# A four-layer float32 decoder trunk on one core: a third deferred column block, another opening order, the last conv chunk without copies, and equal offsets for high and low rows

## The chip, the cores and the metric

The kernel runs on one core of a Trainium2 chip. The metric is the time of one execution on the device in microseconds (us); less is better.

## What is computed

A trunk of four layers over one sequence of 256 rows of 1024 features, float32 throughout. Layer i's mixer is attention (0 and 3), a convolution module (1) or RWKV-7 (2); each is followed by a gated FFN of 2816 hidden units. Each sub-layer is normalised and modulated by six vectors from the conditioning vector c:

```python
for i in range(DEPTH):
    mod = (silu(c) @ ada_w[i] + ada_b[i]).reshape(B, 6, D)
    h = rms_norm(x, norm_mix_g[i]) * (1 + scale_m) + shift_m
    x = x + gate_m * mixer[i % 3](h)
    h = rms_norm(x, norm_ffn_g[i]) * (1 + scale_f) + shift_f
    x = x + gate_f * ((silu(h @ ffn_w_gate[i]) * (h @ ffn_w_up[i])) @ ffn_w_down[i])

def conformer_conv_mixer(h, ...):
    u = glu(h @ w_pw1 + b_pw1)
    u = causal_depthwise_conv(u, w_dw) + b_dw        # 31 taps per channel
    u = layer_norm(u, ln_g, ln_b)
    return silu(u) @ w_pw2 + b_pw2
```

## The kernel before

x lies in SBUF as 8 chunks of 128 features by 256 rows and stays there. Weights come once from HBM, 1 MB at a time, by DMAs issued on SP; each half (128x1024) is split into a high part `wh` (cast to fp32r on ScalarE, ACT, L272) and a low part `wl` = raw - wh (on VectorE, DVE, L273). Activation rows are split in the same way into a high and a low set (`xh`, `xl`; in the FFN's second half `hh`, `hl`). Each exact product is three fp32r passes into one PSUM tile, `wh.xh`, `wh.xl`, `wl.xh` (`mm3`, L289 to L291, with the rows moving and the weights stationary; `mm3t`, L300 to L302, in attention, with the weights moving). Some small products stay float32 in one matmul, which the trace shows as two records.

*Order.* The tile framework's scheduler orders instructions on each engine by the order of the code and by priorities; `issue_after(ins)` keeps an instruction behind another one. `pace` and `pump` spread the steps of c @ ada_w (128x1024 each, L228 on DVE) between the weight blocks.

*Rows and sets.* `new_set` makes a high and a low tile (2048 floats + 48); there are set 0 and set 1. `self.shift` = 16 * i, set by layer i's FFN, moves the place of the rows within them (`chunks`), and the same 16 * i is used in `hh` and `hl`. By this layout the high and the low rows lie 192 bytes apart modulo 1024 in set 1 and in `hh`/`hl`.

*FFN* (`ffn`, L1226). 22 column blocks f, each with a gate half and an up half (24 matmuls each), then 8 output chunks (`w_down`). The first `DEFERRED` = 2 blocks behind a mixer run on rows that aren't yet normalised (set 0; 256 columns and 2 that carry the shift); their results are multiplied by the norm's factor r (L1249, L1252). Meanwhile the normalised rows are built on DVE and ACT into set 1 (L1263 to L1265), which the other blocks use.

*Opening* (`__init__`, `opening`). The first modulation vectors are needed before the first matmul: 512 KB halves of ada_w come in pairs, then x, then more. DVE multiplies each by silu(c). Half the chunks (0 to 3) are scaled, shifted and used in float32 matmuls (L409), while DVE computes the other half of the scale; then chunks 4 to 7 follow as inputs (L388 on ACT) and are split for the first fp32r matmuls (L300).

*Conv* (`conv`, L1062). Eight column blocks d of the first projection give chunks `us[d]`. Depthwise taps run two blocks later (`depthwise`, e = d - 2): 24 taps on TensorE (PE) as matmuls with 32-wide diagonals `dg` over four shifted copies `u4`, which go through DRAM (`shifts`, on GpSimd, POOL); one tap with the bias on ACT; 6 on DVE (L1188). `lead` takes chunk 0's y0 off the others; `tally` (L1096) sums y and its squares for the layer norm, a chain of single DVE and ACT instructions at the end.

## Time and profile before

| | |
|---|---|
| three runs | 1824.60, 1827.16, 1830.43 us (median 1827.16) |
| the profiled execution | 1824.64 us, of it span 1822.8 us |
| mean granted TensorE clock | 0.98 |
| busy | PE 95%, DVE 78%, ACT 54%, POOL 18% |
| DMA | 368 MB, mean 202 GB/s |

The profile is of one execution. A page gives busy time by engine, the span in 40 slices and the costliest groups of instructions. Timelines list instructions with start, duration, line, and in brackets how long the engine had idled before and what released it. A record of a matmul lasts longer than the step from one to the next, since matmuls overlap.

### The profile page before, as it was taken

How to read it: one execution, taken by the hardware profiler on the slowest of the kernel's cores; microseconds unless marked ns; L12 is line 12 of the kernel's file. 1: busy time of each engine (PE TensorE's matmuls, PEld its weight loads, DVE VectorE, ACT ScalarE, POOL GpSimd, SP SyncE). 2: the span in 40 equal slices, each digit the busy share in tenths (PEclk: the TensorE clock that was granted, in tenths of full speed). 3: DMA queues.
4: the chain of work that ended last, by engine and by line, in shares of the span. 5: the costliest groups of instructions: out<-in, count | busy, mean ns of one | idle time of the engine just before them, and what ended most of it. 6: DMA issues, size and time to landing. Idle time of an engine off the chain costs nothing.

```text
span 1822.8 us, 36724 instructions
## 1 busy us (share of the span) xinstructions
PE 1739.8 (95%) x14228; PEld 1645.1 (90%) x14228; DVE 1417.8 (78%) x2826; ACT 977.4 (54%) x2334; POOL 328.3 (18%) x483
## 2 busy tenths in 40 slices
PE   4999999999999899999998999999989999999999
PEld 3999899899997699998887888999989999989999
DVE  6899998977888798777868568877788797786554
ACT  4666565754453464446551346544476676675443
POOL 4645534000004400000000000000054442300000
PEclk8999999999999999999998999999999999999999
DMA  8577666576896448776333104777856554534543
GB/s 340 219 243 267 230 234 229 175 254 237 267 332 197 118 176 311 259 261 233 116 120 106 59 1 144 263 256 239 312 180 216 176 183 158 212 128 165 184 163 114
DMA packets 72686, 368.27 MB, mean 202 GB/s; under 512 B 9392, under 2 KB 11568, under 8 KB 47808
## 3 DMA queue, kind: packets, MB, share of 16 engines
q1 hardware_dynamic: 70592, 360.23, 56.7%
q0 software_dynamic: 1920, 5.70, 1.3%
q8 instruction: 112, 1.84, 0.4%
q14 instruction: 62, 0.51, 0.1%
...
## 4 chain that ended last, share of the span: by engine, by line
PE 55%; DVE 6%; ACT 2%; issue 1%; DMA 0%; POOL 0%; DVEq 0%; ACTq 0%; POOLq 0%
PE pmm L290 12%; PE pmm L289 12%; PE pmm L291 12%; PE pmm L300 3%; PE pmm L301 3%; PE pmm L302 3%; PE pmm L823 1%; PE pmm L923 1%; DVE wl L273 1%; PE aux L595 1%; PE aux L945 1%; PE aux L618 1%; PE aux L937 1%; ACT wh L272 1%; DVE dg L867 1%
## 5 line engine op out<-in xcount | busy, mean ns | idle before, releaser
L272 ACT CAST wh<-raw 128x1024 fp32r<-128x1024 f32 (+2 forms) x501 | 490.2, 982 | 510.7 <-PE pmm L290 273.5
L273 DVE TENSOR_TENSOR wl<-raw,wh 128x1024 fp32r<-128x1024 f32 (+2 forms) x501 | 580.6, 1161 | 184.9 <-ACT wh L272 180.0
L289 PE MATMUL pmm<-xh,wh 128*128 128x256 f32 (+1 forms) x1856 | 522.1, 285 | 15.0 <-ACT xh L1264 6.6
L290 PE MATMUL pmm<-xl,wh 128*128 128x256 f32 (+1 forms) x1856 | 525.5, 285 | 0.1
L291 PE MATMUL pmm<-xh,wl 128*128 128x256 f32 (+1 forms) x1856 | 519.6, 282 | 0.4 <-DVE wl L273 0.4
L289 PEld LDWEIGHTS pmm<-xh,wh 128*128 128x128 f32 x1856 | 350.1, 190 | 21.0 <-ACT xh L306 7.7
L290 PEld LDWEIGHTS pmm<-xl,wh 128*128 128x128 f32 x1856 | 351.5, 190 | 2.2 <-issue 0.8
L291 PEld LDWEIGHTS pmm<-xh,wl 128*128 128x128 f32 x1856 | 351.5, 190 | 1.3 <-DVE wl L273 0.8
L300 PE MATMUL pmm<-wh,xh 128*128 128x256 f32 x1104 | 321.1, 291 | 17.7 <-DVE rope L546 6.8
L302 PE MATMUL pmm<-wl,xh 128*128 128x256 f32 x1104 | 312.2, 284 | 0.8 <-DVE wl L273 0.8
L301 PE MATMUL pmm<-wh,xl 128*128 128x256 f32 x1104 | 312.5, 283 | 0.0
L300 PEld LDWEIGHTS pmm<-wh,xh 128*128 128x128 f32 x1104 | 210.6, 191 | 24.5 <-ACT xh L306 5.9
L228 DVE SCALAR_TENSOR_TENSOR adaw<-adaw,csil 128x1024 f32<-128x1024 f32 x178 | 222.0, 1248 | 4.9 <-DMA adaw<-in_ada_w 4.9
L548 POOL TENSOR_TENSOR rope<-rope,rope 128x128 f32<-128x128 f32 x192 | 147.2, 790 | 427.5 <-ACT wh L272 217.7
L301 PEld LDWEIGHTS pmm<-wh,xl 128*128 128x128 f32 x1104 | 211.5, 192 | 0.1
L302 PEld LDWEIGHTS pmm<-wl,xh 128*128 128x128 f32 x1104 | 210.1, 191 | 1.0 <-DVE wl L273 1.0
L290 PE MATMUL pmm<-hl,wh 128*128 128x256 f32 x704 | 199.1, 283 | 0.0
L291 PE MATMUL pmm<-hh,wl 128*128 128x256 f32 x704 | 197.4, 280 | 0.0
L289 PE MATMUL pmm<-hh,wh 128*128 128x256 f32 x704 | 197.3, 280 | 0.0
L291 PEld LDWEIGHTS pmm<-hh,wl 128*128 128x128 f32 x704 | 132.7, 189 | 0.0
L289 PEld LDWEIGHTS pmm<-hh,wh 128*128 128x128 f32 x704 | 132.6, 188 | 0.0
L290 PEld LDWEIGHTS pmm<-hl,wh 128*128 128x128 f32 x704 | 132.3, 188 | 0.0
...
## 6 DMA issues: line engine op xcount, KB each, us to landing
...
```

Source lines behind the costliest of these rows:

```text
L228: nc.vector.scalar_tensor_tensor(w, w, 1.0, self.csil, ALU.mult, ALU.mult, accum_out=t[:, col:col + 1])
L272: nc.scalar.copy(wh[:, :w], raw)
L273: self.anchor = nc.vector.tensor_sub(wl[:, :w], raw, wh[:, :w].bitcast(F32)).ins
L289: nc.tensor.matmul(out, wh[:, a], xh[:, k, :c], start=first and j == 0, stop=False)
L290: nc.tensor.matmul(out, wh[:, a], xl[:, k, :c], start=False, stop=False)
L291: nc.tensor.matmul(out, wl[:, a], xh[:, k, :c], start=False, stop=last and j == n - 1)
L300: nc.tensor.matmul(out, xh[:, k, tok], wh[:, a], start=first and j == 0, stop=False)
L301: nc.tensor.matmul(out, xl[:, k, tok], wh[:, a], start=False, stop=False)
L302: nc.tensor.matmul(out, xh[:, k, tok], wl[:, a], start=False, stop=last and j == n - 1)
L548: nc.gpsimd.tensor_add(o[:, :, a], o[:, :, a], o2[:, :, c])
L595: nc.tensor.matmul(scs[hh][:, c], T[g][0][rows, hp, tok], T[g][1][rows, hp, kt], start=True, stop=True)
L618: nc.tensor.transpose(pt[:, c * P:(c + 1) * P], pr[:, c * P:(c + 1) * P], self.ident)
```

## The change

1. `DEFERRED` is 3: block f=2 also runs on the deferred rows. The normalised set is still built behind f=0.
2. x is loaded before the first ada_w pair. The low halves of chunks 0 to 3 come behind the last ada step of the opening; the first weight half of the rest is cast before chunks 6 and 7 are made.
3. The conv's last chunk (7) has no shifted copies: 18 taps are float32 matmuls with full 128x128 diagonals `dgs`, built by 18 ACT instructions at d == 2; one tap and the bias stay on ACT, 12 are on DVE. Its taps run at e == 6, before chunk 6's. In the layer norm the mean's square is taken on ACT from PSUM, and the reciprocal root reads the variance directly, with eps as its bias.
4. `self.shift` is gone; tiles of set 0 have 24 floats of pad, those of set 1 none; `hh` and `hl` have 256 floats of pad and the offset 80, 32, 48, 80 by layer. By this layout `xh` and `xl` of set 1, and `hh` and `hl`, lie at equal places modulo 1024 bytes.

```diff
-DEFERRED = 2
+ALONE = 18
+DEFERRED = 3
...
+        nc.sync.dma_start(x, A["x"])
         steps = pair(0)
-        nc.sync.dma_start(x, A["x"])
...
     def chunks(self, t, cols=S):
-        o = self.shift if cols == S else 0
-        return t[:, o:o + KC * cols].rearrange("p (k s) -> p k s", k=KC)
+        return t[:, :KC * cols].rearrange("p (k s) -> p k s", k=KC)
...
-        return self.xp.tile([P, KC * S + 48], dtype, name=f"x{n}{q}")
+        return self.xp.tile([P, KC * S + (0 if q else 24)], dtype, name=f"x{n}{q}")
...
+        if bias is not None:
+            nc.scalar.activation(r, ps, AF.Abs_reciprocal_sqrt, bias=bias)
+            nc.vector.tensor_scalar_add(v, ps, eps)
...
-        split(range(4))
+        with self.tc.issue_after(self.stepped):
+            split(range(4))
...
-            inputs([k])
+            with self.tc.issue_after(self.cast) if k > 5 else nullcontext():
+                inputs([k])
...
+                if d == 2:
+                    for k in range(ALONE):
+                        nc.scalar.mul(dgs[:, k, :], self.ident, wd[:, KC - 1, k:k + 1])
...
-                    shifted[d] = self.shifts(us[d % 4], eye, w4[:, d], tp, dp, shifted.get(d - 1))
+                    if d < KC - 1:
+                        shifted[d] = self.shifts(us[d % 4], eye, w4[:, d], tp, dp, shifted.get(d - 1))
...
+                    if e == KC - 2:
+                        self.depthwise(us[(KC - 1) % 4], None, wd[:, KC - 1], cv[:, 2, KC - 1:], y[:, KC - 1, :],
+                                       tp, (lead, y0), dgs)
...
+            m2 = tp.tile([P, S], F32, name="val")
+            nc.scalar.activation(m2, sums[0], AF.Square, scale=1.0 / D)
             nc.vector.tensor_scalar_mul(mean, sums[0], 1.0 / D)
-            m2 = tp.tile([P, S], F32, name="val")
-            nc.vector.tensor_mul(m2, mean, mean)
...
-        n_pe = 4 * QUADS
+        n_pe = ALONE if dgs is not None else 4 * QUADS
...
+        if dgs is not None:
+            for k in range(n_pe):
+                nc.tensor.matmul(py, dgs[:, k, :], u[:, k:k + S], start=False, stop=k == n_pe - 1,
+                                 skip_group_check=True)
...
-            self.shift = 16 * i
-            hh, hl = (hp.tile([P, FC * S + 48], F32R, name=n)[:, 16 * i:16 * i + FC * S].rearrange(
+            o = (80, 32, 48, 80)[i]
+            hh, hl = (hp.tile([P, FC * S + 256], F32R, name=n)[:, o:o + FC * S].rearrange(
...
-                if f == DEFERRED - 2:
+                if f == 0:
                     dh, dl = self.new_set(1)
```

How the order of instructions moves, at three places. First DVE in the opening, before (`adaw`, `raw` and `wh` hold halves of ada_w; L228 is a step, L307 a low half, L237 the scale):

```order
L307 TENSOR_TENSOR xl0_95<-xh1_228,xh0_94 128x256
L228 SCALAR_TENSOR_TENSOR adaw_171,mod0_0_152<-adaw_171,csil_82 128x1024
L307 TENSOR_TENSOR xl0_95<-xh1_228,xh0_94 128x256
L228 SCALAR_TENSOR_TENSOR raw_173,mod0_0_152<-raw_173,csil_82 128x1024
L307 TENSOR_TENSOR xl0_95<-xh1_228,xh0_94 128x256 x2
L228 SCALAR_TENSOR_TENSOR raw_173,mod0_0_152<-raw_173,csil_82 128x1024
L235 TENSOR_TENSOR mod0_0_152<-mod0_0_152,adab_92 128x4
L228 SCALAR_TENSOR_TENSOR raw_176,mod0_1_155<-raw_176,csil_82 128x1024 x2
L228 SCALAR_TENSOR_TENSOR wh_179,mod0_1_155<-wh_179,csil_82 128x1024
L228 SCALAR_TENSOR_TENSOR wh_181,mod0_1_155<-wh_181,csil_82 128x1024
L235 TENSOR_TENSOR mod0_1_155<-mod0_1_155,adab_92 128x4
L237 SCALAR_TENSOR_TENSOR gs0_1_157<-mod0_1_155,ng_93 128x4
```

and after:

```order
L227 SCALAR_TENSOR_TENSOR adaw_169,mod0_0_152<-adaw_169,csil_82 128x1024
L227 SCALAR_TENSOR_TENSOR adaw_171,mod0_0_152<-adaw_171,csil_82 128x1024
L227 SCALAR_TENSOR_TENSOR raw_173,mod0_0_152<-raw_173,csil_82 128x1024 x2
L234 TENSOR_TENSOR mod0_0_152<-mod0_0_152,adab_92 128x4
L227 SCALAR_TENSOR_TENSOR raw_176,mod0_1_155<-raw_176,csil_82 128x1024 x2
L227 SCALAR_TENSOR_TENSOR wh_179,mod0_1_155<-wh_179,csil_82 128x1024
L227 SCALAR_TENSOR_TENSOR wh_181,mod0_1_155<-wh_181,csil_82 128x1024
L306 TENSOR_TENSOR xl0_95<-xh1_228,xh0_94 128x256
L234 TENSOR_TENSOR mod0_1_155<-mod0_1_155,adab_92 128x4
L306 TENSOR_TENSOR xl0_95<-xh1_228,xh0_94 128x256
L236 SCALAR_TENSOR_TENSOR gs0_1_157<-mod0_1_155,ng_93 128x4
L306 TENSOR_TENSOR xl0_95<-xh1_228,xh0_94 128x256 x4
```

The four low halves that stood between the steps stand behind the last step, and the scale is made between them.

Second DVE in the first FFN, from the last but two pairs of normalised rows on, before (`h0` and `xl1` are the normalised rows, `wl` low halves of weights, `hl` the low half of a block's result):

```order
L307 TENSOR_TENSOR hl_4570<-h_4749,hh_4569 128x256
L1265 SCALAR_TENSOR_TENSOR xl1_4652<-h0_4669,mod0_3_1590,xh1_4651 128x256
L1265 SCALAR_TENSOR_TENSOR xl1_4652<-h0_4673,mod0_3_1590,xh1_4651 128x256
L1263 SCALAR_TENSOR_TENSOR h0_4677<-x_98,gs0_4_2124,rstd2_4613 128x256
L1263 SCALAR_TENSOR_TENSOR h0_4681<-x_98,gs0_4_2124,rstd2_4613 128x256
L273 TENSOR_TENSOR wl_4835<-raw_4828,wh_4834 128x1024
L1265 SCALAR_TENSOR_TENSOR xl1_4652<-h0_4677,mod0_3_1590,xh1_4651 128x256
L1265 SCALAR_TENSOR_TENSOR xl1_4652<-h0_4681,mod0_3_1590,xh1_4651 128x256
L74 TENSOR_TENSOR xl0_95<-shift2_6129,xh0_94 128x8x2
L672 TENSOR_SCALAR omu_10731<-mu_10729 128x48
L273 TENSOR_TENSOR wl_4897<-raw_4894,wh_4896 128x1024
```

and after (`g` and `u` are block f=2's products with r):

```order
L1270 TENSOR_TENSOR g_4822<-pmm_4772,rstd2_4613 128x256
L1286 SCALAR_TENSOR_TENSOR xl1_4652<-h0_4669,mod0_3_1590,xh1_4651 128x256
L1286 SCALAR_TENSOR_TENSOR xl1_4652<-h0_4673,mod0_3_1590,xh1_4651 128x256
L1284 SCALAR_TENSOR_TENSOR h0_4677<-x_98,gs0_4_2124,rstd2_4613 128x256
L1284 SCALAR_TENSOR_TENSOR h0_4681<-x_98,gs0_4_2124,rstd2_4613 128x256
L306 TENSOR_TENSOR hl_4570<-h_4749,hh_4569 128x256
L1286 SCALAR_TENSOR_TENSOR xl1_4652<-h0_4677,mod0_3_1590,xh1_4651 128x256
L1286 SCALAR_TENSOR_TENSOR xl1_4652<-h0_4681,mod0_3_1590,xh1_4651 128x256
L1273 TENSOR_TENSOR u_4828<-pmm_4797,rstd2_4613 128x256
L272 TENSOR_TENSOR wl_4840<-raw_4833,wh_4839 128x1024
L1274 SCALAR_TENSOR_TENSOR h_4823<-u_4828,pmm_4797,g_4822 128x256
L272 TENSOR_TENSOR wl_4902<-raw_4899,wh_4901 128x1024
```

The low half `wl_4835`, which stood before the last pair of normalised rows, has its counterpart `wl_4840` behind them and behind block f=2's `g` and `u`.

Third ACT at the start of the conv, before (`wh` are the casts of the weight halves of blocks d, `sg` a sigmoid, `part` the tap and bias on ACT):

```order
L272 CAST wh_7140<-raw_7138 128x1024
L1112 ACT_TABLE_LOAD
L1112 ACTIVATE sg_7042<-sg_7042,bg_7040 128x256
L272 CAST wh_7144<-raw_7138 128x1024
L1186 ACTIVATE part_7242<-u0_6959,cv_6949,wd_6951 128x256
L272 CAST wh_7255<-raw_7253 128x1024
L1112 ACTIVATE sg_7121<-sg_7121,bg_7119 128x256
L272 CAST wh_7259<-raw_7253 128x1024
L1186 ACTIVATE part_7358<-u1_6960,cv_6949,wd_6951 128x256
L272 CAST wh_7374<-raw_7372 128x1024
L1112 ACTIVATE sg_7200<-sg_7200,bg_7198 128x256
L272 CAST wh_7378<-raw_7372 128x1024
```

and after (L1110 builds the diagonals):

```order
L271 CAST wh_7166<-raw_7164 128x1024
L1110 ACTIVATE dgs_6978<-ident_87,wd_6956 128x128
L1123 ACT_TABLE_LOAD
L1123 ACTIVATE sg_7050<-sg_7050,bg_7048 128x256
L1110 ACTIVATE dgs_6978<-ident_87,wd_6956 128x128 x11
L1123 ACTIVATE sg_7129<-sg_7129,bg_7127 128x256
L1110 ACTIVATE dgs_6978<-ident_87,wd_6956 128x128 x6
L271 CAST wh_7170<-raw_7164 128x1024
L1207 ACTIVATE part_7268<-u0_6966,cv_6954,wd_6956 128x256
L271 CAST wh_7281<-raw_7279 128x1024
L271 CAST wh_7285<-raw_7279 128x1024
```

Eighteen builds stand between the casts `wh_7166` and `wh_7170` of one column block, where one table load and one sigmoid stood between `wh_7140` and `wh_7144`.

## Rows read from the trace of the kernel before

**Rows 1.** The page: busy time by engine, GB/s by slice, the costliest group of matmuls.

```profile
PE 1739.8 (95%) x14228; PEld 1645.1 (90%) x14228; DVE 1417.8 (78%) x2826; ACT 977.4 (54%) x2334; POOL 328.3 (18%) x483
...
GB/s 340 219 243 267 230 234 229 175 254 237 267 332 197 118 176 311 259 261 233 116 120 106 59 1 144 263 256 239 312 180 216 176 183 158 212 128 165 184 163 114
...
L289 PE MATMUL pmm<-xh,wh 128*128 128x256 f32 (+1 forms) x1856 | 522.1, 285 | 15.0 <-ACT xh L1264 6.6
```

**Rows 2.** Windows in the FFN sections: stretch, busy time and records of each engine, granted clock.

```profile
400.00:460.00 60.00, 60.00 (x515) 60.00 (x514) 42.78 (x60) 28.72 (x44) 0.00 (x0) 1.00 0.72 251
480.00:535.00 55.00, 55.00 (x465) 55.00 (x464) 48.81 (x80) 27.63 (x42) 0.00 (x0) 1.00 0.92 323
700.00:780.00 80.00, 80.00 (x675) 80.00 (x674) 61.14 (x89) 37.49 (x57) 0.00 (x0) 1.00 0.79 272
790.00:845.00 55.00, 55.00 (x470) 55.00 (x469) 42.82 (x65) 27.02 (x49) 0.19 (x1) 1.00 0.84 281
1160.00:1240.00 80.00, 80.00 (x681) 80.00 (x680) 59.54 (x83) 38.09 (x58) 0.00 (x0) 1.00 0.77 268
1260.00:1315.00 55.00, 55.00 (x465) 55.00 (x464) 43.16 (x65) 24.59 (x35) 0.00 (x0) 1.00 0.87 298
1660.00:1740.00 80.00, 80.00 (x676) 80.00 (x675) 46.11 (x58) 37.72 (x57) 0.00 (x0) 1.00 0.51 177
```

**Rows 3.** Timeline of PE, attention of layer 0: start, duration, line; first and last of 95.

```profile
101.50 0.28 PE L301 MATMUL pmm<-wh,xl 128*128 128x256 f32 x1
...
112.57 0.28 PE L302 MATMUL pmm<-wl,xh 128*128 128x256 f32 x1
```

**Rows 4.** Timeline of PE, deferred block of the second FFN: first and last of 82.

```profile
659.55 0.47 PE L289 MATMUL pmm<-xh,wh 128*128 128x258 f32 x1
...
669.30 0.28 PE L291 MATMUL pmm<-xh,wl 128*128 128x258 f32 x1
```

**Rows 5.** Waits of PE over the span: total, times, longest.

```profile
PE pmm L289 <- ACT xh L1264: 6.6, 2, 3.3
```

**Rows 6.** Windows behind a wait of PE, opening and first FFN: columns as in rows 2.

```profile
45.00:50.00 5.00, 3.47 (x16) 3.27 (x17) 4.57 (x9) 4.00 (x9) 5.00 (x9) 0.66 0.50 174
361.00:365.00 4.00, 4.00 (x22) 3.91 (x23) 3.97 (x11) 2.33 (x8) 0.00 (x0) 0.62 0.38 154
```

**Rows 7.** Timeline of DVE, opening and first FFN.

```profile
30.54 0.42 DVE L307 TENSOR_TENSOR xl<-xh,xh 128x256 fp32r<-128x256 f32 x1 [2.03 <-ACT xh L306]
...
367.04 1.21 DVE L273 TENSOR_TENSOR wl<-raw,wh 128x1024 fp32r<-128x1024 f32 x1
368.17 0.87 DVE L1265 SCALAR_TENSOR_TENSOR xl<-h,mod,xh 128x256 fp32r<-128x256 f32 x2
```

**Rows 8.** Timeline of PE, first normalised block of the first FFN.

```profile
360.82 1.01 PE L289 MATMUL pmm<-xh,wh 128*128 128x256 f32 x3 [3.29 <-ACT xh L1264]
```

**Rows 9.** Timeline of PE, opening.

```profile
26.39 8.72 PE L409 MATMUL pmm<-raw,xh 128*128 128x256 f32 x32 [9.07 <-ACT xh L388]
34.95 7.07 PE L409 MATMUL aux<-raw,xh 128*128 128x256 f32 x32
45.77 0.39 PE L300 MATMUL pmm<-wh,xh 128*128 128x256 f32 x1 [3.75 <-ACT wh L272]
```

**Rows 10.** Timeline of ACT, opening and start of the conv layer.

```profile
40.61 1.52 ACT L388 ACTIVATE xh<-xl,mod,gs 128x256 f32<-128x256 f32 x2 [8.88 <-DVE gs L237]
...
545.10 1.04 ACT L272 CAST wh<-raw 128x1024 fp32r<-128x1024 f32 x1
```

**Rows 11.** Groups of ACT instructions by line and shape: busy, mean ns, idle before.

```profile
L711 ACT ACTIVATE xl<-raw,mixgs 128x128 f32<-128x128 f32 x16 | 5.1, 391 | 2.0 <-DMA raw<-in_rwkv_aA 2.0
```

**Rows 12.** Timeline of PE, start and end of the conv layer.

```profile
555.91 0.28 PE L291 MATMUL pmm<-xh,wl 128*128 128x258 f32 x1
...
562.25 1.22 PE L1125 MATMUL pmm<-y,lead 128*128 128x256 f32 x2 [2.25 <-DVE y L1189]
...
621.56 2.80 PE L1183 MATMUL pmm<-u,dg 128*32 128x256 f32 x48 [1.23 <-DMA u<-there]
```

More of the change, by code (lines that the diff above doesn't have):

```diff
@@ L148, in __init__ @@
         self.sets = [None, None]
-        self.shift = 0
         for q in range(2):
@@ L227, in ada_step @@
         with self.tc.issue_after(self.anchor) if self.anchor else nullcontext():
-            nc.vector.scalar_tensor_tensor(
-                w, w, 1.0, self.csil, ALU.mult, ALU.mult, accum_out=t[:, col:col + 1])
+            self.stepped = nc.vector.scalar_tensor_tensor(
+                w, w, 1.0, self.csil, ALU.mult, ALU.mult, accum_out=t[:, col:col + 1]).ins
         if col == 0 and m in (1, 4):
@@ L271, in parts @@
         with self.tc.issue_after(self.hold) if self.hold else nullcontext():
-            nc.scalar.copy(wh[:, :w], raw)
+            self.cast = nc.scalar.copy(wh[:, :w], raw).ins
             self.anchor = nc.vector.tensor_sub(wl[:, :w], raw, wh[:, :w].bitcast(F32)).ins
@@ L311, in rsqrt_table, with rsqrt_mean @@
             self.nc.scalar.preload_act_table_set("abs_reciprocal_sqrt_and_small")
-    def rsqrt_mean(self, ps, n, eps, op=ALU.add, rows=P):
+    def rsqrt_mean(self, ps, n, eps, op=ALU.add, rows=P, bias=None):
         nc = self.nc
         v, r, t = (self.sm.tile([P, S], F32, name=m, bufs=1)[:rows] for m in ("var", "rstd", "nrt"))
-        nc.vector.tensor_scalar(v, ps, 1.0 / n, eps, ALU.mult, op)
-        nc.scalar.activation(r, v, AF.Abs_reciprocal_sqrt)
+        if bias is not None:
+            nc.scalar.activation(r, ps, AF.Abs_reciprocal_sqrt, bias=bias)
+            nc.vector.tensor_scalar_add(v, ps, eps)
+        else:
+            nc.vector.tensor_scalar(v, ps, 1.0 / n, eps, ALU.mult, op)
+            nc.scalar.activation(r, v, AF.Abs_reciprocal_sqrt)
         nc.vector.tensor_mul(t, r, r)
@@ L1071, in conv @@
             nc.sync.dma_start(wd, A["w_dw"])
+            eps = hp.tile([P, 1], F32, name="eps")
+            nc.vector.memset(eps, EPS)
             lead = hp.tile([P, P], F32, name="lead")
@@ L1098, in conv @@
             shifted = {}
+            dgs = hp.tile([P, ALONE, P], F32, name="dgs")
             for d in range(KC + 3):
+                if d == 2:
+                    for k in range(ALONE):
+                        nc.scalar.mul(dgs[:, k, :], self.ident, wd[:, KC - 1, k:k + 1])
                 if d < KC:
@@ L1117, in conv @@
                     nc.vector.scalar_tensor_tensor(us[d % 4][:, W - 1:], val, bv, sg, ALU.add, ALU.mult)
[L1118 removed]
+                    if d < KC - 1:
+                        shifted[d] = self.shifts(us[d % 4], eye, w4[:, d], tp, dp, shifted.get(d - 1))
                 if 1 < d <= KC + 1:
                     e = d - 2
[L1121 to L1122 removed]
+                    if e == KC - 2:
+                        self.depthwise(us[(KC - 1) % 4], None, wd[:, KC - 1], cv[:, 2, KC - 1:], y[:, KC - 1, :],
+                                       tp, (lead, y0), dgs)
+                    if e < KC - 1:
+                        self.depthwise(us[e % 4], shifted.pop(e), wd[:, e], cv[:, 2, e:e + 1],
+                                       y[:, e, :] if e else y0, tp, (lead, y0) if e else None)
                     if e == 0:
@@ L1170, in shifts, with depthwise @@
         return u4, dg, last.ins
-    def depthwise(self, u, shifted, w, bias, y, tp, less):
+    def depthwise(self, u, shifted, w, bias, y, tp, less, dgs=None):
         nc = self.nc
         W = w.shape[-1]
-        n_pe = 4 * QUADS
-        u4, dg, self.copied = shifted
+        n_pe = ALONE if dgs is not None else 4 * QUADS
         py = self.ps.tile([P, 512], F32, name="pmm")[:, :S]
@@ L1180, in depthwise @@
             nc.tensor.matmul(py, *less, start=True, stop=False, skip_group_check=True)
-        for q in range(QUADS):
-            for g in range(4):
-                nc.tensor.matmul(py[32 * g:32 * g + 32, :], dg[:, 4 * q + g, :], u4[:, g, 4 * q:4 * q + S],
-                                 start=q == 0 and not less, stop=q == QUADS - 1, skip_group_check=True)
+        if dgs is not None:
+            for k in range(n_pe):
+                nc.tensor.matmul(py, dgs[:, k, :], u[:, k:k + S], start=False, stop=k == n_pe - 1,
+                                 skip_group_check=True)
+        else:
+            u4, dg, self.copied = shifted
+            for q in range(QUADS):
+                for g in range(4):
+                    nc.tensor.matmul(py[32 * g:32 * g + 32, :], dg[:, 4 * q + g, :], u4[:, g, 4 * q:4 * q + S],
+                                     start=q == 0 and not less, stop=q == QUADS - 1, skip_group_check=True)
         part = tp.tile([P, S], F32, name="part")
```

4 lines of the change are left out of this document (1 added, 3 removed).

## The prediction

> **What bounds the kernel now.** I read the page's busy table first: the reader is to see TensorE (PE) busy for 1739.8 us, 95% of the span [rows 1]. Only two things can therefore shorten the run: the places where PE stands or runs at half clock, and the time of one matmul. For the second I read seven stretches of the feed-forward (FFN) sections, gate/up of all four and down of three, each with PE 100% busy at a granted clock of 1.00 [rows 2]. Counts there include the two or three matmuls that reach over an edge (each record lasts 0.28 us and they start 0.12 us apart), so I take off 2.4. One 128x256 fp32r matmul then takes 117.1 ns in gate/up of the first section (60 / 512.6), 118.9, 117.9 and 118.8 in the next three; in down it takes 118.9, 117.6 and 118.9. The code is the same in the four; what differs is the offset, 16 floats more from section to section, at which the moving rows lie. Offset thus decides up to 1.5% of a matmul's time, and there are 3 x 1856 matmuls with moving x rows [rows 1] and, by the loops of down, 3 x 22 x 8 x 4 = 2112 with moving h rows: 7680. Third, the waits: two of 3.3 us each where an FFN section changes from the deferred rows to the normalised ones, in the sections behind the two attentions [rows 5, 8]; one of 3.75 us in the opening [rows 9]; one of 2.25 us at the conv's start and one of 1.23 at its end [rows 12]. After the first two kinds PE runs for 3 to 4 us at half clock: 1.2 instead of 2.4 GHz, seen as a mean of 0.66 over 45 to 50 us and of 0.62 over 361 to 365 us [rows 6].
>
> **Third deferred block.** DVE is what PE waits for at 360.82: DVE works without a gap and finishes the last pair of normalised low rows at 368.17 + 0.87 = 369.04, while PE runs over them [rows 7]. Before, block f=2 needs those rows; it starts at 360.82 [rows 8], loses 4 x 0.38 = 1.5 us to the clock [rows 6], and with 48 matmuls at 0.118 (5.66 us) blocks f=2 to f=5 end at 368.0, 373.7, 379.3 and 385.0. After, f=2 runs on the deferred rows straight behind f=1 (357.4 to 363.1), so gap and half clock go: 3.3 + 1.5 = 4.8 at most. But PE now comes to the normalised rows while DVE is still at them, and the two extra multiplies by the norm's factor (g and u, 0.43 each as the pair of row operations at 368.17) stand ahead of the low half of f=3's second weight, wl_4840. The last low rows come at 369.04 - 1.2 (the wl that stood ahead of them, at 367.04 [rows 7], now comes behind) + 0.43 = 368.3, the u multiply at 368.7, wl_4840 at 369.9; its 24 matmuls end at 372.7, f=4 at 378.4, f=5 at 384.0. That is 1.0 less; since the matmuls ahead of wl_4840 have then run with PE and its clock up, and the g multiply falls into DVE's earlier pauses at best, I take **1.5 in each of two sections, -3.0**. The two sections behind conv and rwkv don't stand among these waits and are costed at nothing: DVE's work there hides behind PE's. Bounds: -9.6 (both stalls whole) and +1.7 (nothing gained, and 2 x 0.86 us of multiplies on the path).
>
> **Opening.** x (1 MB) is moved ahead of the first two halves of ada_w (1 MB). At the 340 GB/s of the span's first slice [rows 1] these come up to 3.1 us later, x as much earlier. The scale behind them releases PE's first 64 records (32 matmuls), at 26.39 [rows 9]. DVE idles between its first steps, so I take less than half, 1.3 later: 27.7. These matmuls take until 34.95 + 7.07 = 42.02, 15.6 us in all, so they end at 43.3. DVE's second list of ada steps loses four low-half subtractions (0.4 each) and the 2.03 us wait for ACT at 30.54 [rows 7]: 3.7 less, 1.3 more, so the scale that frees ACT at 40.61 [rows 10] comes 2.4 earlier, at 38.2. From there to the first fp32r matmul it was 5.2 us, of which the inputs of chunks 6 and 7 (about 2.1 with their casts) now stand behind the weight's cast: ready at 41.3. PE is then the later one and goes on at 43.3 without standing: 45.77 - 43.3 = 2.5, and the half clock goes with the wait, 5 x 0.34 = 1.7. I take **-4.0**; bounds -5.5 (x's move costs nothing) and +1 (3.1 late, and the wait stays).
>
> **Conv, start.** Eighteen 128x128 diagonals are built on ACT; the nearest row is a 128x128 scaling, 391 ns [rows 11], 7.0 us in all. They stand on ACT between the two weight casts of column block d=2, of which the second, at 545.10, had come with 5 us to spare [rows 10]. After, about 7.6 us stand before it (the builds and two sigmoids): cast near 552.9, its low half near 555.2 on DVE, where PE wanted it at about 553 (the block's last matmul starts at 555.91 [rows 12], its second half is 24 of 0.12). So PE stands 2.1 and then loses some 1.5 to the half clock that follows such a stand [rows 6], 3.6 together; but the 2.25 us that PE waits for DVE's y right behind [rows 12] is then mostly covered. Net **+1.8**; bounds 0 and 7.0.
>
> **Conv, end.** Chunk 7's copies through DRAM go, and with them PE's wait of 1.23 us and 24 small matmuls, 2.80 [rows 12]. Eighteen fp32 matmuls of 128x128 by 256 come; from the opening's rows one takes 7.07 / 16 = 0.44 [rows 9], 7.9 in all, but they need only u, and run ahead of chunk 6's, in the place of waits. Twelve taps on DVE (six before) lie beside them. By my count the last y comes 1.1 later, and the reciprocal root straight from the variance gives 0.25 back: **+0.85**; bounds -1 and +4.2 (7.9 - 2.8 - 1.2, and 0.3 more of waits). POOL's memsets, five DMAs less, and mu's load one section later are covered by POOL's idle 82% of the span [rows 1] and cost nothing; without that cover the third layer's first mixes, which need mu, would start later.
>
> **Addresses.** The high and low rows now lie at equal offsets, where they were 192 bytes apart. No row shows that for moving rows of x or h. In attention the moving operands are the weight's high and low half, which lie at equal offsets: 95 matmuls from 101.50 to 112.57, 117.8 ns each [rows 3]. I take 117.8, as the nearest case, for gate/up from f=3 (19 x 48 x 4 = 3648, mean now 118.2) and for down (2112, mean 118.5): -1.5 and -1.5, **-3.0**. Bounds: at 117.1 -7.0, at 118.9 +3.4.
>
> A rule that speaks against this term: the Trainium skill, "TensorE: Matmul & The Clock Gate", Part 2 (step 1), gives TensorE two independent read ports and says that loading the next tile's weights takes no read bandwidth from the running matmul; no address would matter, the term would be 0 and the sum 3.0 higher. The spread of 117.1 to 118.9 among equal code in [rows 2] speaks against it.
>
> **Sum.** -3.0 - 4.0 + 1.8 + 0.85 - 3.0 = -7.4. The profiled execution took 1824.64 us, so 1817.3 by its own clock; it stands 2.5 below the median of the runs, 1827.16. Against that median the time is 1819.8; I say 1820.
>
> **Rivals.**
> *All matmuls with moving x or h run at 117.1.* Speaks for it: the first section shows that such a place exists. gate/up and down gain 7.0, the other 5568 - 3648 = 1920 (conv, rwkv, deferred blocks) up to 1.5 ns, 2.9: -9.9 for -3.0, so 1813.
> *Addresses do nothing* (equal offsets only shift who is slow): 1823.
> *DVE becomes the bound at the FFN starts.* It is without a gap there [rows 7]; if wl comes later by what f=2 gave, the term is +1.7 for -3.0: 1824.5.
> *Equal offsets are the bad case.* If high and low rows at one offset hinder each other, all 7680 matmuls with moving x or h pay. The slowest long stretch of such matmuls is the deferred block, 81 steps from 659.55 to 669.30, 120.4 ns [rows 4]; against a mean of 118.2 that is +16.9 for -3.0: 1839.7, slower than before. It decides from 118.8 ns on (118.2 + 4.4 us, the gain of all other terms, over 7680); attention's equal weights at 117.8 speak against it.
> *The conv's builds and matmuls stay on the path:* 7.0 + 4.2 for 2.65: 1828.3. That is also where the change fails to do what it says, the copies' wait exchanged for as long a row of matmuls.
>
> **How the numbers follow.** About 0.3%, 5.5 us, is what a measurement of this kernel tells from no change; faster means under 1821.7, slower over 1832.7. Forecast 0.54, own range 1814 to 1825, a good two thirds of it faster (0.39, same 0.15); all at 117.1 0.13, faster; addresses nothing 0.06, same; DVE bound 0.14 (0.12 same, 0.02 slower with a second mishap); bad offsets 0.08, slower; conv on the path 0.05 (0.03, 0.02). Faster 0.52, same 0.36, slower 0.12. The range: from 1806 (the first rival with the opening's best) to 1829 (the conv rival); left out are the bad offsets and tails, 0.15.
>
> **What would show it.** Opening: the first fp32r matmul near 43.3 without an idle bracket, clock 1.00 over 43 to 48. FFN of the first and last layer: 144 matmuls in a row, then short waits for xl and wl, no 0.62. Conv: a wait for ACT's wh or DVE's wl in block d=2; no wait for u from DRAM; 18 matmuls in about 8 us near 614. Addresses: the seven stretches of [rows 2] near 117.8, alike in all layers. I'm wrong if the gap at f=2 reappears whole at f=3, if PE still waits at the first fp32r matmul of the opening, or if the seven stretches move by more than 1 ns on the mean.

## Result and profile after

The changed kernel takes 1801.81 us (median of 4 runs, 1798.57 to 1806.48) against 1827.71 before (4 runs): ratio 0.9861, 95% interval 0.9833 to 0.9889. It was forecast at 1820, with a range from 1806 to 1829: the sign was right, the gain is 26 us instead of 8.

The profiled execution took 1798.57 us. The page's busy line, against [rows 1]: PE is busy for 22.4 us less with nearly the same work.

```profile
PE 1717.4 (96%) x14216; PEld 1623.9 (90%) x14216; DVE 1420.0 (79%) x2840; ACT 984.0 (55%) x2357; POOL 331.7 (18%) x477
```

The windows in the four FFN sections, gate/up, then down, of each. Columns are as in [rows 2]: the stretch, its length, busy time and records of PE, of its weight loads, of DVE, ACT and POOL, then the granted clock, the DMA share and GB/s.

```profile
400.00:455.00 55.00, 55.00 (x488) 55.00 (x487) 40.83 (x56) 27.03 (x41) 1.08 (x1) 1.00 0.70 247
490.00:520.00 30.00, 30.00 (x267) 30.00 (x266) 27.24 (x44) 15.89 (x24) 0.00 (x0) 1.00 0.93 353
700.00:765.00 65.00, 65.00 (x576) 65.00 (x575) 52.40 (x77) 31.97 (x49) 0.00 (x0) 1.00 0.81 281
785.00:825.00 40.00, 40.00 (x335) 40.00 (x335) 30.21 (x46) 17.11 (x28) 0.19 (x1) 1.00 0.85 284
1160.00:1235.00 75.00, 75.00 (x665) 75.00 (x664) 58.05 (x82) 37.43 (x56) 0.00 (x0) 1.00 0.76 263
1255.00:1300.00 45.00, 45.00 (x385) 45.00 (x384) 35.15 (x55) 20.23 (x30) 0.00 (x0) 1.00 0.89 303
1660.00:1725.00 65.00, 65.00 (x576) 65.00 (x575) 39.66 (x51) 32.05 (x48) 0.00 (x0) 1.00 0.52 180
1740.00:1790.00 50.00, 50.00 (x443) 50.00 (x443) 26.35 (x33) 19.54 (x25) 0.00 (x0) 1.00 0.48 162
```

With 2.5 taken off each count (0.28 us over steps of 0.113), a matmul takes 113.3 ns in gate/up of all four sections (55 / 485.5), where it took 117.1 to 118.9, and 113.4 and 113.5 in down of the first and last. In down of the second and third it takes 120.3 and 117.6. None of the rows of before showed a step below 117.

Where the 26 us lie, from starts in the two timelines (x's last update closes a mixer or an FFN; f=5 is taken by its silu on ACT, y0 by its first matmul in PE):

| stage | before | after | difference |
|---|---|---|---|
| to the first fp32r matmul | 45.77 | 42.13 | -3.6 |
| rest of the first attention | 301.99 | 299.31 | -2.7 |
| FFN starts to f=5, four sections | 35.52, 34.11, 33.81, 35.80 | 33.83, 34.87, 33.78, 31.22 | -1.7, +0.8, 0.0, -4.6 |
| gate/up f=5 to f=21, sum of four | 362.1 | 347.3 | -14.8 |
| down, sum of four | 259.5 | 253.9 | -5.7 |
| conv to y0 | 24.02 | 27.79 | +3.8 |
| conv, y0 to the last of its first projection | 47.43 | 47.66 | +0.2 |
| conv, from there to its second projection | 21.79 | 23.93 | +2.1 |
| conv's second projection | 26.35 | 25.34 | -1.0 |
| rwkv, second attention, tail | 594.6 | 595.8 | +1.2 |

In this profile the matmul step carries 20.5 of the 26. How far that is a matter of chance, and which of the small differences are noise, the experiments show.

### The profile page after: what moved, and what is told of

It reads as the page before. It is cut to its first block, busy times and chain, and to the rows that moved or that the text cites. A ratio compares the mean times of both kernels' runs of the same rounds, so it can differ in the third digit from the quotient of the medians.

```text
span 1796.8 us, 36742 instructions
## 1 busy us (share of the span) xinstructions
PE 1717.4 (96%) x14216; PEld 1623.9 (90%) x14216; DVE 1420.0 (79%) x2840; ACT 984.0 (55%) x2357; POOL 331.7 (18%) x477
## 4 chain that ended last, share of the span: by engine, by line
PE 55%; DVE 9%; ACT 3%; issue 2%; DMA 0%; POOL 0%; DVEq 0%; ACTq 0%; SPq 0%; POOLq 0%
PE pmm L288 11%; PE pmm L290 11%; PE pmm L289 11%; PE pmm L299 3%; PE pmm L301 3%; PE pmm L300 3%; DVE wl L272 2%; PE pmm L928 1%; PE pmm L1204 1%; PE aux L600 1%; ACT wh L271 1%; PE aux L623 1%; PE aux L950 1%; PE aux L942 1%; PE pmm L828 1%
## 5 line engine op out<-in xcount | busy, mean ns | idle before, releaser
L289 PE MATMUL pmm<-xl,wh 128*128 128x256 f32 (+1 forms) x1856 | 518.2, 280 | 0.2 <-DVE xl L1286 0.2
L227 DVE SCALAR_TENSOR_TENSOR adaw<-adaw,csil 128x1024 f32<-128x1024 f32 x178 | 222.2, 1250 | 4.6 <-DMA adaw<-in_ada_w 4.5
```

The lines of the kernel that those rows point to most:

```text
L227: self.stepped = nc.vector.scalar_tensor_tensor(w, w, 1.0, self.csil, ALU.mult, ALU.mult, accum_out=t[:, col:col + 1]).ins
L289: nc.tensor.matmul(out, wh[:, a], xl[:, k, :c], start=False, stop=False)
```

## Experiments

Three theories of the matmul step are tried. Theory 1: the start of the moving operand modulo 512 bytes sets it. Theory 2: it is good when high and low rows lie at equal places. Theory 3, formed on the way: the distance between the starts of the moving and the stationary operand sets it.

**Addresses alone, and all but the addresses.** `addr_only` is the kernel before with the hunks on `shift`, `chunks`, `memory` and `o` alone; `no_addr` the changed kernel without them.

> The kernel before with the fourth part of the change alone (tiles without shift, new pads and offsets). Theory 1 (the start of a moving operand modulo 512 bytes sets its matmul's time; nothing else of the change touches it): gate/up blocks from f=3 on fall from 5.62-5.71 to 5.44 us in all four FFN sections, down falls to 7.5 us per output chunk in the first and last section and stays near 7.85 in the other two; in all about -20 us against before, near 1807. Rival (the matmul step fell because the other parts changed what DVE, ACT and the DMAs do beside it): steps as before, 117 to 119 ns, and a time within 3 us of before.

> The changed kernel with the addresses of before (shift 16*i, pad 48), so the third deferred block, the opening and the conv part alone. Theory 1: about -5.5 us against before, near 1822: opening -6.3, FFN starts -5, conv +6, and steps of 117 to 119 ns again. Rival (the other parts made the matmuls faster): near 1802, steps of 113.3 ns.

`addr_only`: 1807.17 us (1802.55 to 1818.8), ratio 0.9891 (0.9864 to 0.9919), -21 us against the 1828.56 of the kernel before beside it. `no_addr`: 1822.21, ratio 0.9971 (0.9952 to 0.999), -6. Together that is the result. The rival is out: without the addresses gate/up of the first two sections stays at 116.9 and 118.9 ns.

```profile
400.00:455.00 55.00, 55.00 (x473) 55.00 (x472) 39.50 (x53) 25.68 (x40) 0.00 (x0) 1.00 0.71 247
700.00:765.00 65.00, 65.00 (x549) 65.00 (x549) 49.33 (x73) 30.89 (x46) 0.00 (x0) 1.00 0.82 286
```

But `addr_only` shows something new in its gate/up windows, first to last section:

```profile
400.00:455.00 55.00, 55.00 (x488) 55.00 (x486) 40.50 (x55) 27.47 (x41) 0.00 (x0) 1.00 0.74 255
700.00:765.00 65.00, 65.00 (x555) 65.00 (x554) 51.02 (x75) 30.93 (x46) 0.00 (x0) 1.00 0.78 268
1160.00:1235.00 75.00, 75.00 (x664) 75.00 (x663) 57.72 (x81) 36.99 (x56) 0.00 (x0) 1.00 0.77 268
1670.00:1735.00 65.00, 65.00 (x554) 65.00 (x553) 38.56 (x50) 30.90 (x46) 0.00 (x0) 1.00 0.49 169
```

113.3, 117.6, 113.4 and 117.9 ns, though the rows lie at the same place in all four.

**Another offset in the second and third FFN.**

```diff
-            o = (80, 32, 48, 80)[i]
+            o = 80
```

> The changed kernel with offset 80 for hh and hl in all four layers, so both start at 512 modulo 1024 bytes everywhere (before 320 in the second layer's FFN, 384 in the third's). Theory 1 (start modulo 512): down of the second and third FFN falls from 7.86 and 7.78 to 7.50 us per output chunk, 8 x 0.64 = about 5 us less than the changed kernel, near 1797. Theory 2 (what counts is that high and low rows lie at equal places): they were equal already, no difference.

1801.82 us (1796.29 to 1803.71), ratio 0.9849 (0.9824 to 0.9873): no difference, as theory 2 said. The profile says otherwise. Gate/up and down of the second FFN, then of the third:

```profile
700.00:765.00 65.00, 65.00 (x555) 65.00 (x554) 51.02 (x75) 30.93 (x46) 0.00 (x0) 1.00 0.81 283
790.00:825.00 35.00, 35.00 (x299) 35.00 (x299) 27.73 (x42) 15.69 (x23) 0.00 (x0) 1.00 0.85 296
1160.00:1235.00 75.00, 75.00 (x665) 75.00 (x664) 57.82 (x82) 37.54 (x56) 0.00 (x0) 1.00 0.76 267
1260.00:1300.00 40.00, 40.00 (x355) 40.00 (x354) 31.77 (x51) 18.48 (x27) 0.00 (x0) 1.00 0.88 308
```

Down of the third fell to 113.5 as forecast. In the second the whole section, gate/up too, ran at 117.6 to 118.0, at an address at which the first profile showed 113.3. One execution isn't enough to judge an offset: the levels must be read section by section.

**Which place is good.** Two kernels with other `o`: `scan_equal`, and `scan_mixed` with `hh` and `hl` apart.

```diff
-            o = (80, 32, 48, 80)[i]
+            o = (16, 240, 224, 208)[i]
```

```diff
-                "p (f s) -> p f s", f=FC) for n in ("hh", "hl"))
+                "p (f s) -> p f s", f=FC) for n, o in zip(("hh", "hl"), ((80, 32), (32, 80), (80, 208), (16, 80))[i]))
```

> The changed kernel with high and low rows of the FFN's second half at equal places, but another in each section: 256, 128, 64 and 0 modulo 1024 bytes in the four. Theory 1 (start on a multiple of 512 bytes): only the fourth section's down can run at 7.48 us per output chunk, the others at 7.75 to 7.95; if 256 is grain enough, the first too. Theory 2 (equal places): all four can run at 7.48. Gate/up is as in the changed kernel: 5.44 us per block where the section locks into the fast level, 5.65 where not.

> The changed kernel with high and low rows of the FFN's second half at unequal places: 512/320, 320/512, 512/0 and 256/512 modulo 1024 bytes in the four sections (high/low). Theory 1: the third section's down (both on multiples of 512, not equal) can run at 7.48 us per output chunk; the first, with two passes of three on a multiple of 512, and the second, with one of three, stay above 7.7. Theory 2: none runs at 7.48, the third like the first.

Down of the four sections, `scan_equal` (1811.71 us):

```profile
485.00:520.00 35.00, 35.00 (x311) 35.00 (x310) 31.48 (x54) 17.87 (x28) 0.00 (x0) 1.00 0.95 348
790.00:830.00 40.00, 40.00 (x342) 40.00 (x341) 29.81 (x47) 18.14 (x30) 0.19 (x1) 1.00 0.86 291
1270.00:1305.00 35.00, 35.00 (x294) 35.00 (x294) 27.70 (x44) 15.31 (x23) 0.00 (x0) 1.00 0.89 302
1760.00:1800.00 40.00, 40.00 (x342) 40.00 (x342) 21.23 (x27) 15.94 (x21) 0.00 (x0) 1.00 0.46 150
```

`scan_mixed` (1810.59 us):

```profile
490.00:525.00 35.00, 35.00 (x296) 35.00 (x295) 30.53 (x51) 17.02 (x26) 0.00 (x0) 1.00 0.92 325
800.00:840.00 40.00, 40.00 (x342) 40.00 (x341) 30.97 (x48) 20.86 (x40) 0.19 (x1) 1.00 0.82 278
1265.00:1305.00 40.00, 40.00 (x356) 40.00 (x355) 32.06 (x51) 18.95 (x28) 0.00 (x0) 1.00 0.86 307
1760.00:1800.00 40.00, 40.00 (x342) 40.00 (x341) 20.27 (x25) 15.67 (x20) 0.00 (x0) 1.00 0.44 146
```

113.5, 117.8, 120.1, 117.8 and 119.3, 117.8, 113.2, 117.8. Equal places give 120.1 with both at 64; unequal ones 113.2 at 512 and 0. So theory 2 falls; theory 1 held so far, with a grain of 256. The last section of each is not against it: its gate/up ran at 5.65 us per block too, the slower level.

**The weights' place.** 192 bytes are set aside ahead of the weight tiles. `w0` keeps the places of set 1, `hh` and `hl`; `best2` is `w0` with the conv chunk through the copies and `o = 208`.

```diff
+        cp.tile([P, 48], F32, name="shove")
...
-        return self.xp.tile([P, KC * S + (0 if q else 24)], dtype, name=f"x{n}{q}")
+        return self.xp.tile([P, KC * S + (0 if q else 128)], dtype, name=f"x{n}{q}")
```

> The changed kernel with 192 bytes set aside ahead of the weight tiles, so the weights' halves start at 0 instead of 832 modulo 1024 bytes; the deferred set is padded so that it starts at 0 and 512 and all others stay. In attention the weights are the moving operand. Theory 1: attention's fp32r matmuls (3312, 117.8 ns) can fall to 113.3, up to 15 us less in all, near 1790; FFN levels as in the changed kernel. Rival (the matmul's step hangs on the place of the stationary operand as well, or on the distance between the two): FFN steps leave 113.3, and the time goes up by 10 us or more.

> The changed kernel with the weights on multiples of 1024 as in the run before, hh and hl at 0 in all layers, and the last conv chunk through the copies. Theory 1: -15 us in attention, -3 in the conv, -5 in the two FFN sections whose rows lay off the grain: 1780 to 1787, below both kernels. Rival (levels are chance, and addresses only shift who is slow): within 5 us of the changed kernel.

`w0`: 1833.73 us (1831.23 to 1844.75), ratio 1.0043 (1.0025 to 1.0061): 32 us slower than the changed kernel. `best2`: 1829.12, ratio 1.0016 (0.9998 to 1.0035), where 1780 to 1787 was forecast. Theory 1 fell here. Gate/up and down of the first FFN in `w0`, moving rows on multiples of 512:

```profile
400.00:455.00 55.00, 55.00 (x461) 55.00 (x460) 38.64 (x53) 25.88 (x40) 0.00 (x0) 1.00 0.68 236
490.00:520.00 30.00, 30.00 (x253) 30.00 (x252) 26.86 (x44) 14.72 (x24) 0.00 (x0) 1.00 0.90 315
```

120.0 and 119.8 ns. Put together by the **distance** from the stationary operand's start to the moving one's, modulo 256 bytes (the layout has the weights at 64 in the changed kernel, at 0 in `w0`), all rows so far in which high and low rows have one distance fit: 0 gives 120, 64 gives 117.8, 192 gives 113.3 or 117.8. That is theory 3. Where the two differ the step isn't the mean: 192 for `hh` and 0 for `hl` (the first section of `scan_mixed`) took 119.3. The second and third section of `w0`, at 64 and 128, took 117.9 and 118.5 in down.

**The distance.** `w0_rel` leaves the weights of `w0`, moves set 1 by 48 floats, and puts `hh` and `hl` at the distance 192 (first and last FFN) or 128. `rel`, of which the diff shows the main lines, gives set 1, `hh`, `hl` and attention's operands the distance 192 (not the deferred blocks, whose chunks are 258 columns long); `best3` is `rel` with the conv chunk through the copies. `scan_fine` is the changed kernel with `o = (8, 216, 12, 20)[i]`.

```diff
-    def chunks(self, t, cols=S):
-        return t[:, :KC * cols].rearrange("p (k s) -> p k s", k=KC)
+    def chunks(self, t, cols=S, q=1):
+        o = (48 if q else 16) if cols == S else 0
+        return t[:, o:o + KC * cols].rearrange("p (k s) -> p k s", k=KC)
...
-            o = (80, 32, 48, 80)[i]
+            o = 0
```

> The weights at 0 modulo 256, as in the run that was slower, and the moving x rows of set 1 at 192, hh and hl at 192 in the first and last FFN and at 128 in the other two. Theory 3 (distance): gate/up can lock at 5.44 us per block again, down at 7.48 us per chunk in the first and last FFN, 7.83 (118.6 ns) in the other two. Theory 1 (moving start modulo 512): nothing at 5.44 or 7.48, since no moving operand starts on a multiple of 512.

> The changed kernel with hh and hl at distances from the weights of 160, 224, 176 and 208 bytes modulo 256 in the four sections' down. Theory 3 asks for the width of the good place: if the grain is 64 bytes, 208 and 224 behave as 192 (7.48 possible), 160 and 176 as 128 (7.83); if only exactly 192 is good, all four stay above 7.7.

> The changed kernel with every moving operand placed 192 bytes behind the stationary one modulo 256: x rows for attention at 128 (weights stay at 64, all modulo 256), set 1, hh and hl at 0. Theory 3 (formed on the runs so far: the distance of moving and stationary operand modulo 256 bytes decides; 0 gives 120 ns, 64 gives 117.7, 128 118.6, and 192 alone lets a stretch lock at 113.3): attention's fp32r matmuls can fall from 117.8 to 113.3 (up to 15 us), down of the second and third FFN to 7.48 us per output chunk (5 us); 1782 to 1795. Theory 1 (start of the moving operand modulo 512): attention as before, as the weights stay at 832; down gains its 5 us; near 1797.

> The kernel of the run before it (all distances 192 modulo 256), with the last conv chunk through the DRAM copies as in the kernel before the change. Theory 3 with the conv stage's cost of 6 us as read from the traces: 3 to 6 us less than that run, 1777 to 1792, below both kernels. Rival: the conv stage's cost comes back elsewhere, no difference.

`w0_rel` (1803.78 us), gate/up and down of the first FFN (192), down of the second and third (128):

```profile
400.00:455.00 55.00, 55.00 (x487) 55.00 (x487) 40.70 (x56) 27.53 (x42) 0.00 (x0) 1.00 0.74 248
490.00:520.00 30.00, 30.00 (x267) 30.00 (x266) 26.62 (x43) 15.70 (x25) 0.00 (x0) 1.00 0.94 338
800.00:830.00 30.00, 30.00 (x255) 30.00 (x254) 22.86 (x36) 14.83 (x27) 0.19 (x1) 1.00 0.87 296
1265.00:1300.00 35.00, 35.00 (x297) 35.00 (x296) 27.27 (x43) 15.43 (x22) 0.00 (x0) 1.00 0.87 297
```

113.5 (55 / 484.5), 113.4, 118.8, 118.8: with the weights elsewhere the good place has moved with them, and the step of 113 is back. `scan_fine` (1815.38 us), down at 160, 224, 176, 208:

```profile
490.00:525.00 35.00, 35.00 (x300) 35.00 (x300) 31.57 (x52) 18.04 (x28) 0.00 (x0) 1.00 0.92 335
790.00:830.00 40.00, 40.00 (x341) 40.00 (x340) 30.10 (x46) 20.34 (x38) 0.19 (x1) 1.00 0.81 276
1275.00:1310.00 35.00, 35.00 (x296) 35.00 (x295) 27.82 (x43) 15.38 (x23) 0.00 (x0) 1.00 0.88 296
1765.00:1800.00 35.00, 35.00 (x296) 35.00 (x296) 18.00 (x22) 13.92 (x18) 0.00 (x0) 1.00 0.49 160
```

117.6, 118.2, 119.3, 119.3, while gate/up, at 192, ran at 5.44 us per block in all four sections of this profile. Of the eight distances tried only 192 shows 113; the four of `scan_fine` were seen in one section each.

`rel`: 1797.72 us (1785.8 to 1801.56), ratio 0.9838 (0.9808 to 0.9869), 4 less than the changed kernel by the medians, not up to 20, and not told apart by the intervals. Down came out as forecast: 61.9 us in the second and third section for 65.4 and 64.2. Attention's matmuls did speed up, but the second attention takes only 2.6 us less (306.7 for 309.3). Windows in it, the changed kernel's and then `rel`'s:

```profile
1318.00:1334.00 16.00, 16.00 (x137) 16.00 (x136) 15.78 (x30) 11.10 (x54) 9.91 (x9) 1.00 0.67 240
```

```profile
1318.00:1334.00 16.00, 16.00 (x143) 16.00 (x143) 16.00 (x30) 11.77 (x55) 10.55 (x9) 1.00 0.70 243
```

143 records for 137. But DVE is busy for 16.00 of 16 us, and PE's waits in the first attention for the rotary step (`rope`) on POOL and DVE grew from 6.6 and 4.6 us to:

```profile
PE aux L586 <- POOL rope L579: 9.1, 7, 3.6
PE pmm L300 <- DVE rope L552: 5.9, 4, 2.6
```

That attention now takes what DVE and POOL take is argued from these rows, not shown by a run. `best3`: **1785.64 us** (1778.87 to 1790.78), ratio 0.9774 (0.9757 to 0.9791), 39 us below the 1824.4 of the kernel before beside it, and faster than the changed one by intervals that don't touch. It lies 12 below `rel`, where 3 to 6 was forecast; its conv is 5.4 shorter (24.4 us to y0, 22.3 at the end), so the rest isn't explained.

**The other parts.** `no_chunk7` takes back the last conv chunk's part (not the layer norm's); `late_dgs` builds the diagonals in fours, each behind a weight cast of blocks 3 to 7; `defer2` sets `DEFERRED = 2`; `open_old` takes back the opening.

> The changed kernel with the last conv chunk through the DRAM copies as before (no 18 diagonals, no reordering of chunks 6 and 7); the layer norm part stays. Theory (the 18 builds on ACT and the 18 float32 matmuls cost 4.0 us at the conv's start and 2.1 at its end): 5 to 6 us faster than the changed kernel, near 1796, with no wait for wh in block d=2 and the wait of 1.2 us for the copies back. Rival (PE would wait at the conv's start for DVE's first y anyway, and at the end for the copies): within 1.5 us of the changed kernel.

> The changed kernel with the 18 diagonals built in fours behind the weight casts of blocks 3 to 7 instead of ahead of block 2's. Theory (4 of the conv's 6 us are the builds ahead of a cast, 2 the matmuls at the end): from the FFN's last update to the first y in PE 24 us as before instead of 27.8, the end as in the changed kernel; about 4 us faster than it. Rival (the casts wait for other things as well): the start stays at 26 us or more.

Start and end of the conv in the changed kernel (PE):

```profile
539.40 0.58 PE L288 MATMUL pmm<-xh,wh 128*128 128x258 f32 x1 [2.67 <-ACT wh L271]
...
552.24 0.99 PE L1141 MATMUL pmm<-y,lead 128*128 128x256 f32 x2 [2.81 <-DVE y L1210]
```

```profile
604.67 7.94 PE L1198 MATMUL pmm<-u,dgs 128*128 128x256 f32 x36
...
612.97 2.80 PE L1204 MATMUL pmm<-u,dg 128*32 128x256 f32 x48
...
623.83 1.01 PE L288 MATMUL pmm<-xh,wh 128*128 128x256 f32 x3 [5.27 <-ACT xh L305]
```

and ACT ahead of the first of these:

```profile
532.95 3.32 ACT L1110 ACTIVATE dgs<-ident,wd 128x128 f32<-128x128 f32 x11
...
536.57 1.85 ACT L1110 ACTIVATE dgs<-ident,wd 128x128 f32<-128x128 f32 x6
538.33 1.03 ACT L271 CAST wh<-raw 128x1024 fp32r<-128x1024 f32 x1
```

The cast that PE waits for at 539.40 stands behind 17 of the 18 builds (11 and 6, 0.31 us each). At the end 36 records, 18 matmuls, take 7.94 us. `no_chunk7`: 1799.15 us (1796.07 to 1803.04), ratio 0.984 (0.9816 to 0.9864), against 0.9861: 2.7 us less by the medians, which the intervals don't tell apart, while its conv takes 23.8 us to y0 and 21.6 at the end, 6.3 less than the changed kernel's. Its profile came 3.0 us later to the end of the first attention, whose code is the same; over nine profiles with this opening and attention that stage ends between 341.4 and 344.8, and the changed kernel's first profile is the earliest of them. `late_dgs`: 1803.38 (1794.31 to 1816.96), ratio 0.9877 (0.9846 to 0.9907), not told apart by time; y0 comes after 25.7, not 24 or 27.8, and PE no longer waits for a cast but for DVE:

```profile
546.35 4.48 PE L1205 MATMUL pmm<-u,dg 128*32 128x256 f32 x48 [2.54 <-DVE part L1210]
551.48 0.70 PE L1142 MATMUL pmm<-y,lead 128*128 128x256 f32 x2 [0.64 <-DVE y L1211]
```

So the builds' place was worth 2.1 us, and the end stayed at 23.93. The costs of the conv part hold over the profiles: y0 comes after 27.3 to 29.0 us in the twelve with the builds ahead of block 2's cast, after 23.8 to 25.3 in the five with the copies. The end is less sure: 23.9 in all thirteen with the diagonals, 21.6 to 22.4 in four of the five with the copies, but 25.4 in the fifth (`best2`).

> The changed kernel with two deferred blocks again. Theory (the third block takes away the stand and the half clock at the start of the normalised rows): the wait of 3.3 us for xh and a mean clock near 0.6 behind it come back in the first and last FFN; from the last update of the mixer to the silu of f=5 it takes 1.5 us more in the first FFN, 3 to 4.5 more in the last, up to 1 less in the second; 4 to 6 us slower than the changed kernel. Rival (DVE is the bound there, two blocks or three): within 2 us.

> The changed kernel with the opening of before (x behind the first pair, low halves between the steps, all inputs before the first cast). Theory: the first fp32r matmul comes at 45.5 instead of 42.1 us with a wait for wh and half clock behind it, and the first attention's 192nd matmul of that kind about 3.6 us later; 3 to 5 us slower in all. Rival (attention's later waits for rope and DVE take it up): the stage to the last update of attention differs by less than 1.5 us.

`defer2`: 1813.33 us (1805.02 to 1818.31), ratio 0.9923 (0.9901 to 0.9946), 8 to 12 us more than the changed kernel by the medians of its two sets of runs (the second is below), more than the 4 to 6 of the forecast; the interval clears the first set's, not the second's (0.9865 to 0.9913). The starts to f=5 take 36.98, 33.56, 33.34 and 35.89: +3.2, -1.3, -0.4, +4.7 against the changed kernel, 6 in all, of which 0.6 may be the slower level in each of the first and last section, as both ran at it in this profile. The wait is back whole:

```profile
PE pmm L288 <- ACT xh L1285: 6.6, 2, 3.3
```

`open_old`: 1808.47 (1804.21 to 1816.68), ratio 0.9912 (0.9892 to 0.9932). The first fp32r matmul is at 45.48 behind a wait, as before:

```profile
45.48 0.58 PE L299 MATMUL pmm<-wh,xh 128*128 128x256 f32 x1 [2.62 <-ACT wh L271]
```

and x's last update in attention at 345.93, 4.5 later than in the changed kernel's first profile, 1.9 later than in its second, 1.2 later than in the latest of the nine. The time, 3 to 7 us more than the changed kernel's two sets by the medians, agrees in sign; what of the opening's gain is left at the end of attention is shown only as 1 to 4.5 us.

**The changed kernel once more.**

> The changed kernel once more. Theory 3 with chance (at the good distance of 192 bytes a stretch locks at 113.3 or at 117.7 ns, by how the streams meet at its start): the same instructions and addresses can show a section at 5.65 us per block which the first profile shows at 5.44. Rival (the level is fixed by the program): four sections at 5.44 again, times within 3 us of each other.

1805.57 us (1800.0 to 1812.92), ratio 0.9889 (0.9865 to 0.9913). Gate/up of the second and of the last FFN:

```profile
720.00:770.00 50.00, 50.00 (x427) 50.00 (x426) 38.73 (x59) 23.95 (x36) 0.00 (x0) 1.00 0.74 261
1665.00:1735.00 70.00, 70.00 (x597) 70.00 (x596) 41.77 (x54) 33.39 (x50) 0.00 (x0) 1.00 0.51 173
```

117.8 and 117.7 ns, where the same program showed 113.3. So at a distance of 192 a section runs at one of two levels, by chance. Of 56 gate/up sections at 192 in 14 profiles 43 ran at 5.44 us per block and 13 at 5.65; none changed level between its f=5 and f=21. A section at the slower level costs 17 x 0.21 = 3.6 us and, where down has that distance too, 2.5 more (64.35 us for 61.89). So the stage table is in part luck: all four of its sections ran at the faster level, as in 6 of the 14 profiles. In this second profile gate/up gained 8.0 us on the kernel before and down 3.1, 11 for 20.5. Four sections, at up to 6 us each, come near the spread of these kernels from run to run (7 to 23 us), so medians 3 us apart don't tell two of them apart; the kernel before spreads by 13 to 14 us as well, so the levels aren't all of it. What decides the level at a section's start stays open. At the places of before no such change was seen: the four sections took 5.60, 5.69, 5.64 and 5.69 us per block in the profile of before and again in that of `no_addr`.

## Why the prediction was wrong

*The matmul step* (forecast -3.0; measured -20.5 in the first profile, -11 in the second, -21 by the medians of `addr_only`): the failing step is "I take 117.8, as the nearest case", with "at 117.1 -7.0" as the far bound. It took the offset as a property of the moving rows alone, because in [rows 2] only they moved; the weights stood at one place through the whole trace, so no row of before could show a distance of 192 for both halves. (By the layout the high h rows of the first section lay at 192, the low ones at 128, and down took 118.9 there.) What the runs show in its place: the distance of both operands sets the step, and 192 gives 113.3. The spread within equal code was read rightly, as a sign that places matter, but its smallest value is no bound for places not seen. The rival "all matmuls run at 117.1" pointed the right way and lay 4 ns per matmul short. "Equal offsets" were not the cause in either direction: they can be good (113.3) or bad (120).

The rule of the Trainium skill weighed there ("TensorE: Matmul & The Clock Gate", Part 2, step 1) says that loading the next tile's weights takes no read bandwidth from the running matmul. These runs don't agree: at a granted clock of 1.00 the step goes from 113.3 to 120.0 ns when the weights move and the FFN's rows stay (`w0`), and back when the rows follow (`w0_rel`). That the two reads hinder each other is the nearest explanation; no run shows the reads themselves.

*Opening* (-4.0, of it 2.5 to the first fp32r matmul and 1.7 in the clock behind it): -3.6 to that matmul, and -5.5 at the 48th (48.26 for 53.77). Right in its mechanism: the wait and the half clock are gone, as the row and the window behind it show (against the 45.77 and 0.66 of [rows 6, 9]). x's move cost 0.2 us (the first float32 matmuls start at 26.61 for 26.39), not 1.3:

```profile
42.13 0.47 PE L299 MATMUL pmm<-wh,xh 128*128 128x256 f32 x1
```

```profile
43.00:48.00 5.00, 4.94 (x41) 4.74 (x40) 4.65 (x8) 5.00 (x21) 5.00 (x9) 1.00 0.61 198
```

*Third deferred block* (-1.5 in each of two sections): -1.7 and -4.6 against before, -3.2 and -4.7 against `defer2`, where nothing else differs (0.6 of each may be the level). In the first section DVE's late xl and wl took a part of the gain back, as said:

```profile
361.18 0.38 PE L288 MATMUL pmm<-xh,wh 128*128 128x256 f32 x1 [0.44 <-ACT xh L1285]
361.77 0.39 PE L289 MATMUL pmm<-xl,wh 128*128 128x256 f32 x1 [0.20 <-DVE xl L1286]
...
363.63 0.38 PE L290 MATMUL pmm<-xh,wl 128*128 128x256 f32 x1 [0.96 <-DVE wl L272]
```

In the last section no wait of PE has a bracket, and the gain came near the bound of 4.8. DVE has three ada steps (L227, 3.7 us) between 341 and 369 us, and none in the same stretch of the last section; that they are the cause is argued, not shown. It was wrong to take both sections as one. The second section lost 0.8 (1.3 by `defer2`) where nothing was costed.

*Conv* (+1.8 and +0.85): +3.8 and +2.1. The late cast and the row of matmuls are as forecast, but both overlaps failed. The builds took 5.6 us, not 7.0. At the start the late cast (2.67 us of wait) and the wait for y0 (2.81 where it was 2.25, [rows 12]) both stayed: DVE's low half starts at 539.39, behind the cast, the taps behind it, and y is made at 551.78, so the second wait isn't cover for the first. At the end the 18 matmuls are PE's whole work from 604.67 to 612.6, with chunk 6's 24 behind them, and there was no wait there for them to fill.

*POOL's moves and mu* (nothing): rwkv took 281.7 us before and 282.9 after; in sixteen of the eighteen profiles it lies between 279.8 and 283.8, so no cost is shown. In the other two, `scan_fine` and `w0`, it took 294.7 and 295.3: the granted clock was 0.60 to 0.73 over 60 us and more there (0.64 and 0.60 over 980 to 1040 us in `scan_fine`), where the changed kernel's profile has 0.67 and 1.00. Which of the two an execution gets is not explained.

*The sum.* Without the addresses the terms came to -4.35; `no_addr` measured -6.4 by the medians, -2 to -9 by its interval. That this is near is in part luck: in the stage table the conv cost 3.3 more than forecast, and the FFN starts gave 2.5 more. Two smaller slips: the range's lower end doesn't follow from its own words (1813 less the opening's further 1.5 is 1811.5, not 1806), and the 120.4 ns of [rows 4], used for the rival of bad offsets, is for 258 columns, not 256.
